# Rotary embedding on one core: half a row less of a cast ahead of the copy that releases a store

## The chip, the core and the metric

The kernel runs on one core of a Trainium2 chip. Its time is the device time of one execution in microseconds (us). Before the change the median of three runs is 161.36 us (161.2 to 161.51).

## The reference

Each row of x has 16 heads of 64 numbers. The first 32 of a head (x1) are turned against the last 32 (x2) by an angle that depends only on the row's place in the sequence:

```python
batch, seq, dim = 16, 512, 1024        # x is float32; cos and sin are [512, 32]
x = x.reshape(batch, seq, num_heads, head_dim)
x1, x2 = x[..., :half_dim], x[..., half_dim:]
rotated = np.concatenate([x1 * cos - x2 * sin, x1 * sin + x2 * cos], axis=-1)
```

So 33.5 MB are read, 33.5 MB are written, and there are a few operations for each number.

## The kernel before

**Tiling.** Two batches make a slab: 8 rows of 1024 numbers on each of 128 partitions, 8192 float32 numbers (32 KB) a partition, 4 MB in all. There are 8 slabs, 0 to 7. Two slabs make a pair, and SBUF has three places for a pair (a tile each, named `pair`). Pairs 0-1, 2-3 and 4-5 have a place of their own; pair 6-7 comes into the place of pair 0-1, so its load must wait until store 0-1 has landed.

**The work of a slab.** It is done inside the slab's own place. ScalarE casts the float32 numbers to bf16 into the lower half of the slab (`cast`). VectorE multiplies by the sine table into the upper half, then by the cosine table in the lower half (both line 170), and adds the two with the halves of each head exchanged (line 173). ScalarE then copies the bf16 result of the upper half back over the whole slab as float32 (`copy_out`). Both ScalarE steps go through the helper `copy`, so all of them have line 154. The tables are built once, at the start, with a few small matmuls.

**Transfers.** SP issues all loads and stores through the helper `issue` (line 66), in program order: load 0, the two tables, load 1, loads 2-3 and 4-5 as one transfer each, all within the first 4.3 us; then store 0-1, load 6-7, stores 2-3, 4-5 and 6-7, each of these in two halves (even partitions, then odd ones) of 4 MB.

**Order around the change.** ScalarE's and SP's orders are written out by hand (`keep_in_program_order`). Each pass of the loop first casts the next slab and then copies out its own: in the pass of slab 1, ScalarE casts slab 2, and then copies slab 1 (on which VectorE's three operations have run) in two pieces. The piece held back is the last row (`LAST[1]`, 1024 numbers a partition), and between the two pieces ScalarE casts the first `PART` numbers of slab 3. Store 0-1 waits for the last row. The rest of slab 3's cast comes at the start of the next pass (slab 2), and VectorE's work on slab 3 waits for all of that cast. Pair 2-3 has a like arrangement: the last 512 numbers of slab 3's copy (`LAST[3]`) come only in the pass of slab 4, and store 2-3 waits for them.

The lines that carry this:

```python
    LAST = {1: dim, 3: dim // 2}
...
                    cast(v, PART if v[0] == 3 else 0)
...
            copy_out(u, 0, n * dim - LAST[s])
            cast((3, 0, rpp), 0, PART)
            copy_out(u, n * dim - LAST[s])
```

Of the kernel before, what the change touches and what calls it, by code (L numbers as in the profile page):

```python
# [2 lines left out]

# [4 lines left out]


@with_exitstack  # L10
def kernel(
    ctx: ExitStack,
    tc: tile.TileContext,
    x: bass.AP,
    cos: bass.AP,
    sin: bass.AP,
    num_heads: int,
    out: bass.AP,
):
    nc = tc.nc  # L20
    P = nc.NUM_PARTITIONS

    batch, seq, dim = x.shape
    nh = num_heads
    hd = dim // nh
    half = hd // 2
    bf16 = mybir.dt.bfloat16
    f32 = mybir.dt.float32

    nb = 2  # L30
    nslabs = batch // nb
    rpp = nb * seq // P
    W = rpp * dim
    TP = seq // (2 * rpp)
    TS = P // TP
    TW = 2 * rpp * half

    out_flat = out.rearrange("b s h d -> b s (h d)")

    singles = ctx.enter_context(tc.tile_pool(name="singles", bufs=1))  # L40
    pairs = ctx.enter_context(tc.tile_pool(name="pairs", bufs=3))
    psum = ctx.enter_context(tc.tile_pool(
        name="psum", bufs=1, space=bass.MemoryType.PSUM))


    def view(t, offset, *dims):
        return dataclasses.replace(t, offset=t.offset + offset,
                                   ap=[t.ap[0], *[list(d) for d in dims]])

    places = [pairs.tile([P, 2 * W], f32, tag="pair", name="pair") for _ in range(3)]


    def here(s, n=1):
        return view(places[s // 2 % 3], s % 2 * W, (1, n * W))


    def there(t, s, n=1):  # L60
        return bass.AP(tensor=t.tensor, offset=t.offset + s // 2 * 2 * P * W + s % 2 * W,
                       ap=[[2 * W, P], [1, n * W]])


    def issue(out, in_):
        tc.keep_in_program_order(nc.sync.dma_start(out=out, in_=in_))  # L66


    def load(s, n=1, parts=slice(None)):
        issue(here(s, n)[parts], there(x, s, n)[parts])  # L70


    def store(s, n=1, parts=slice(None)):
        issue(there(out_flat, s, n)[parts], here(s, n)[parts])


    EVEN, ODD = slice(0, P, 2), slice(1, P, 2)


    load(0)  # L80


    cos_sb = singles.tile([P, TW], f32, tag="cos_sb")
    sin_sb = singles.tile([P, TW], f32, tag="sin_sb")
    for t, src in ((cos_sb, cos), (sin_sb, sin)):
        nc.vector.memset(t, 0.0)  # L86
        issue(t[::TS], bass.AP(
            tensor=src.tensor, offset=src.offset, ap=[[TW, TP], [1, TW]]))

    load(1)  # L90
    for s in (2, 4):
        load(s, 2)


    pick = singles.tile([P, 2 * P], bf16, tag="pick")
    nc.gpsimd.memset(pick, 0.0)  # L96
    for g in range(2):
        part = view(pick, g * P, (TP, P // TP), (1, TP))
        nc.gpsimd.affine_select(  # L99
            out=part, in_=part, compare_op=mybir.AluOpType.not_equal,  # L100
            fill=1.0 - 2.0 * g, base=0, pattern=[[0, P // TP], [-TS, TP]],
            channel_multiplier=1)

    tab1 = singles.tile([P, 2 * TW], bf16, tag="tab1")
    for i, t in enumerate((cos_sb, sin_sb)):
        nc.vector.tensor_copy(out=view(tab1, i * TW, (1, TW)), in_=t)  # L106

    accs, tabs = [], []
    for h in range(2):
        acc = psum.tile([P, 2 * rpp * hd], f32, tag=f"acc{h}", name="acc")  # L110
        for i in range(2):
            for f in range(2):
                nc.tensor.matmul(  # L113
                    view(acc, i * rpp * hd + f * half, (hd, rpp), (1, half)),
                    view(pick, i * f * P, (1, P)),
                    view(tab1, i * TW + h * rpp * half, (half, rpp), (1, half)),
                    start=True, stop=True)
        accs.append(acc)
        tabs.append(singles.tile([P, 2 * rpp * hd], bf16, tag=f"tab{h}", name="tab"))
    nc.vector.tensor_copy(out=tabs[0], in_=accs[0])  # L120

    PART = 2 * dim
    LAST = {1: dim, 3: dim // 2}
    passes = []
    for s in range(nslabs):
        r = 0
        for n in {0: (4, 4), nslabs - 1: (4, 2, 2)}.get(s, (rpp,)):  # L130
            passes.append((s, r, n))
            r += n


    def halves(u):
        s, r, n = u
        t = here(s).bitcast(bf16)
        return [view(t, (2 * r + i * n) * dim, (1, n * dim)) for i in range(2)]


    def cast(u, a=0, b=None):
        s, r, n = u
        m = (n * dim if b is None else b) - a
        copy(view(halves(u)[0], a, (1, m)), view(here(s), r * dim + a, (1, m)))


    def copy_out(u, a=0, b=None):
        s, r, n = u
        m = (n * dim if b is None else b) - a
        copy(view(here(s), r * dim + a, (1, m)), view(halves(u)[1], a, (1, m)))  # L150


    def copy(out, in_):
        tc.keep_in_program_order(nc.scalar.copy(out=out, in_=in_))  # L154


    for i, u in enumerate(passes):
        s, r, n = u
        if i == 0:
            cast(u)  # L160
            cast(passes[1])
            copy(tabs[1], accs[1])
            cast(passes[2])
        elif s > 0 and not r:
            for v in passes:
                if v[0] == s + 1:
                    cast(v, PART if v[0] == 3 else 0)
        lo, up = halves(u)
        for t, a in ((up, 0), (lo, rpp * hd)):
            nc.vector.tensor_mul(  # L170
                out=t, in0=lo,
                in1=view(tabs[s % 2], a + r * hd, (hd, n), (0, nh), (1, hd)))
        nc.vector.tensor_add(  # L173
            out=up, in0=up, in1=view(lo, half, (hd, n * nh), (-half, 2), (1, half)))

        if s == 1:
# [3 lines that stand above are left out]
            for act in (store, load):  # L180
                for parts in (EVEN, ODD):
                    act(0 if act is store else 6, 2, parts)
        elif s == 3:
            copy_out(u, 0, n * dim - LAST[s])
        else:
            copy_out(u)
        if s == 4:
            copy_out((3, 0, rpp), rpp * dim - LAST[3])
            for parts in (EVEN, ODD):
                store(2, 2, parts)  # L190
        elif s > 4 and s % 2 and r + n == rpp:
            for parts in (EVEN, ODD):
                store(s - 1, 2, parts)


# [1 line left out]
_INS = ['x', 'cos', 'sin', 'num_heads']  # L197
_OUTS = [((16, 512, 16, 64), 'float32')]

_NUMBERS = {'num_heads': 16}  # L200


# [26 lines left out]
```

## Time and profile before

| What | Number |
|---|---|
| time, median of three runs | 161.36 us |
| the profiled execution: its time | 161.71 us |
| the profiled execution: its span | 159.9 us |
| ScalarE (ACT) busy | 114.3 us, 71% of the span |
| VectorE (DVE) busy | 109.6 us, 69% |
| TensorE (PE) busy | 1.9 us, 1% |
| bytes moved by DMA | 67.24 MB, 420 GB/s over the span |

The profile is of one execution. Its span runs from the first to the last instruction; its time is 1.8 us longer, with what lies around the span. Times within the profile count from the span's start. "Busy" says how long an engine had work, not whether anyone waited for that work; that is read from the chain of waits and from the landing times of the transfers. Transfers are issued by SP, which takes about half a us for each; the bytes move afterwards, on 16 DMA engines, and a transfer's time "to landing" runs from its issue to the moment when its last byte is there, with whatever it stood in the queue.

### The profile page before, as it was taken

To read this page: it belongs to the slowest core of one execution; us is meant where nothing else is said; L and a number is where in the kernel's file an instruction comes from. 1 tells how busy PE (TensorE), PEld (TensorE's weight loads), DVE (VectorE), ACT (ScalarE), POOL (GpSimd) and SP (SyncE) were. 2 spreads that over 40 slices of the span, in tenths; PEclk is the share of its full clock that TensorE was granted. 3 is DMA by queue.
4 is the path that set the end of the run, shared out by engine and by line. 5 is a ranking of instruction groups with operands and counts; after the bars stand their busy time and mean duration, and the time that the engine had idled before them with its cause. 6 is when DMAs were issued, how large, how long until landed. Compare 5 with 4: busy or idle time off the path is not lost.

```text
span 159.9 us, 176 instructions
## 1 busy us (share of the span) xinstructions
PE 1.9 (1%) x8; PEld 1.1 (1%) x8; DVE 109.6 (69%) x38; ACT 114.3 (71%) x27; POOL 1.1 (1%) x7
## 2 busy tenths in 40 slices
PE   0004000000000000000000000000000000000000
PEld 0002000000000000000000000000000000000000
DVE  2004899999806998999899999909999998000000
ACT  3008949992499999999999995699999969400000
POOL 2000000000000000000000000000000000000000
DMA  7999999979989697996996996996996996997966
GB/s 262 393 393 443 500 402 524 475 311 524 410 377 524 262 524 311 475 525 279 508 525 262 525 524 262 525 508 279 524 508 279 524 492 295 525 443 344 525 262 262
DMA packets 1472, 67.24 MB, mean 420 GB/s; under 512 B 256, under 2 KB 256, under 8 KB 320
## 3 DMA queue, kind: packets, MB, share of 16 engines
q1 hardware_dynamic: 1472, 67.24, 98.0%
HBM read 33.69 MB, written 33.55 MB: 420 GB/s over the span
## 4 chain that ended last, share of the span: by engine, by line
DMA 51%; DVE 14%; ACT 12%; issue 6%; ACTq 2%; SPq 1%
DMA pair<-in_x_dram 36%; DMA out_dram<-pair 15%; ACT pair L154 12%; DVE pair L170 10%; DVE pair L173 4%; ACTq L224 1%; SPq L66 1%; DVE sin_sb L86 0%; DVE cos_sb L86 0%; ACTq L154 0%
## 5 line engine op out<-in xcount | busy, mean ns | idle before, releaser
L154 ACT CAST pair<-pair 128x8192 bf16<-128x8192 f32 (+10 forms) x25 | 112.2, 4557 | 22.7 <-DMA pair<-in_x_dram 21.3
L170 DVE TENSOR_TENSOR pair<-pair,tab 128x8192 bf16<-128x8192 bf16 (+2 forms) x22 | 71.4, 3258 | 12.4 <-ACT pair L154 12.0
L173 DVE TENSOR_TENSOR pair<-pair 128x8192 bf16<-128x8192 bf16 (+2 forms) x11 | 35.8, 3259 | 0.3
L106 DVE CAST tab<-cos_sb 128x512 bf16<-128x512 f32 x1 | 0.4, 426 | 11.1 <-DMA cos_sb<-in_cos_dram 11.1
L113 PE MATMUL acc<-tab,pick 128*128 128x256 bf16 x8 | 1.9, 412 | 13.5 <-DVE tab L106 13.5
L120 DVE CAST tab<-acc 128x1024 bf16<-128x1024 f32 x1 | 1.2, 1225 | 1.0 <-PE acc L113 1.0
L154 ACT ACT_TABLE_LOAD x1 | 1.3, 1283 | 0.7 <-PEq L210 0.7
L113 PEld LDWEIGHTS <-pick 128*128 128x128 bf16 x8 | 1.1, 137 | 13.8 <-issue 12.0
L86 DVE MEMSET cos_sb<- 128x512 f32 x1 | 0.5, 485 | 0.9 <-PEq L210 0.9
L154 ACT CAST tab<-acc 128x1024 bf16<-128x1024 f32 x1 | 1.0, 1005 | 0.0
L99 POOL TENSOR_SCALAR_AFFINE_SELECT pick<-pick 128x128 bf16<-128x128 bf16 x2 | 0.6, 308 | 0.1
L86 DVE MEMSET sin_sb<- 128x512 f32 x1 | 0.5, 485 | 0.1
L106 DVE CAST tab<-sin_sb 128x512 bf16<-128x512 f32 x1 | 0.4, 419 | 0.0
L96 POOL MEMSET pick<- 128x256 bf16 x1 | 0.3, 311 | 0.3 <-POOLq L210 0.3
L210 POOL MEMSET const-bfloat16-1.0<- 128x1 bf16 x1 | 0.1, 101 | 0.0
L210 POOL MEMSET const-uint8-127<- 128x1 uint8 x1 | 0.1, 101 | 0.0
L210 POOL MEMSET const-float32-0.0<- 128x1 f32 x1 | 0.1, 98 | 0.2 <-issue 0.2
L210 POOL MEMSET const-float32-1.0<- 128x1 f32 x1 | 0.1, 98 | 0.0
## 6 DMA issues: line engine op xcount, KB each, us to landing
pair<-in_x_dram SPq DMA_DIRECT2D x2, 4096.0 KB, 16.1
out_dram<-pair SPq DMA_DIRECT2D x8, 17.9
cos_sb<-in_cos_dram SPq DMA_DIRECT2D x1, 64.0 KB, 11.5
sin_sb<-in_sin_dram SPq DMA_DIRECT2D x1, 64.0 KB, 11.1
pair<-in_x_dram SPq DMA_DIRECT2D x4, 29.1
```

Of the source, the lines that this page charges most:

```text
L66: tc.keep_in_program_order(nc.sync.dma_start(out=out, in_=in_))
L86: nc.vector.memset(t, 0.0)
L96: nc.gpsimd.memset(pick, 0.0)
L99: nc.gpsimd.affine_select(out=part, in_=part, compare_op=mybir.AluOpType.not_equal, fill=1.0 - 2.0 * g, base=0, pattern=[[0, P // TP], [-T ...
L106: nc.vector.tensor_copy(out=view(tab1, i * TW, (1, TW)), in_=t)
L113: nc.tensor.matmul(view(acc, i * rpp * hd + f * half, (hd, rpp), (1, half)), view(pick, i * f * P, (1, P)), view(tab1, i * TW + h * rpp * ...
L120: nc.vector.tensor_copy(out=tabs[0], in_=accs[0])
L154: tc.keep_in_program_order(nc.scalar.copy(out=out, in_=in_))
L170: nc.vector.tensor_mul(out=t, in0=lo, in1=view(tabs[s % 2], a + r * hd, (hd, n), (0, nh), (1, hd)))
L173: nc.vector.tensor_add(out=up, in0=up, in1=view(lo, half, (hd, n * nh), (-half, 2), (1, half)))
L210: nc = _bacc.Bacc("TRN2", target_bir_lowering=False, num_devices=1)
L224: with _tile.TileContext(nc) as tc:
```

## The change

One line. ScalarE casts the first 1536 numbers of slab 3 (one and a half rows) instead of the first 2048 (two rows) between the two pieces of the copy of slab 1. The rest of the cast, in the next pass, has 6656 numbers instead of 6144. The number and the order of instructions stay as they were on all engines; only these two sizes differ.

```diff
-    PART = 2 * dim
+    PART = 3 * dim // 2
     LAST = {1: dim, 3: dim // 2}
```

## The prediction

> **What bounds the kernel now.** I read the profile in this order: the DMA queue, the chain of waits, then stretches of time, because the last two seem to say different things. The queue's row on the page:
>
> ```profile
> q1 hardware_dynamic: 1472, 67.24, 98.0%
> ```
>
> One queue moves all 67.24 MB, and its packets fill 98.0% of the time of 16 DMA engines. The chain that ended last (start, length, what):
>
> ```profile
> 49.12 8.91 ACT pair L154 x3
> 58.04 0.02 issue
> 58.05 0.53 SPq L66
> 58.58 0.04 issue
> 58.62 23.34 DMA out_dram<-pair
> 81.96 0.02 issue
> 81.98 0.02 SPq L66
> 82.00 0.04 issue
> 82.04 19.12 DMA pair<-in_x_dram
> ```
>
> It runs through exactly the edited place: the three ScalarE pieces from 49.12 (seven rows of slab 1 out, two rows of slab 3 in, the last row of slab 1 out), then store 0-1, then load 6-7. Taken literally, a store issued earlier ends everything earlier. But the 23.34 us run from the issue to the landing, and a packet that waits its turn counts in them. So I ask when the transfers landed (the DMA view of three single issues, the last number being us to landing): load 4-5, issued at 3.79; the first half of store 0-1, issued at 58.05; and the very first load, issued at 0.74, which has nothing ahead of it.
>
> ```profile
> pair<-in_x_dram SPq DMA_DIRECT2D x1, 58.6
> ```
> ```profile
> out_dram<-pair SPq DMA_DIRECT2D x1, 14.1
> ```
> ```profile
> pair<-in_x_dram SPq DMA_DIRECT2D x1, 4096.0 KB, 12.0
> ```
>
> Load 4-5 lands at 3.79 + 58.6 = 62.4, that is 4.35 us after the store was issued. The store's first half (4 MB) lands at 58.05 + 14.1 = 72.1, its second at 58.62 + 23.34 = 81.96. The rest of the kernel but the last 8 MB, cut at those and the later landing times (columns: stretch, length, then each engine's busy time, clock, DMA share, GB/s):
>
> ```profile
> 42.17:49.10 6.93, 0.00 (x0) 0.00 (x0) 1.06 (x1) 6.90 (x1) 0.00 (x0) 1.00 1.03 435
> 49.10:62.41 13.31, 0.00 (x0) 0.00 (x0) 13.09 (x3) 13.31 (x5) 0.00 (x0) 1.00 0.98 404
> 62.41:81.96 19.55, 0.00 (x0) 0.00 (x0) 18.26 (x6) 19.55 (x4) 0.00 (x0) 1.00 0.99 429
> 81.96:101.16 19.20, 0.00 (x0) 0.00 (x0) 19.03 (x5) 16.07 (x4) 0.00 (x0) 1.00 1.01 437
> 101.16:120.52 19.36, 0.00 (x0) 0.00 (x0) 14.87 (x4) 19.28 (x5) 0.00 (x0) 1.00 1.00 433
> 120.52:139.83 19.31, 0.00 (x0) 0.00 (x0) 14.71 (x10) 15.89 (x5) 0.00 (x0) 1.00 1.00 434
> ```
>
> Each stretch from 62.41 on moves 8 MB in 19.2 to 19.55 us with a DMA share of 0.99 to 1.01: the engines have no gap to close. From the landing of load 4-5 to the last landing at 159.10 are 96.69 us for ten transfers of 4 MB, 9.67 each. **The bytes bound the kernel**, one after the other; the chain goes through the store because its wait is the last one named, not because the DMA engines stood idle for it.
>
> **The change, step by step.** ScalarE's order stays; two of its pieces change size. The rows, by form (busy, mean ns):
>
> ```profile
> L154 ACT CAST pair<-pair 128x7168 f32<-128x7168 bf16 x1 | 6.2, 6160 | 0.0
> ...
> L154 ACT CAST pair<-pair 128x2048 bf16<-128x2048 f32 x3 | 5.6, 1892 | 0.0
> L154 ACT CAST pair<-pair 128x6144 bf16<-128x6144 f32 x1 | 5.3, 5306 | 0.0
> ...
> L154 ACT CAST pair<-pair 128x1024 f32<-128x1024 bf16 x1 | 1.0, 1039 | 0.0
> ```
>
> 1. *The cast ahead of the last row* goes from 2048 to 1536 elements. No row has 1536; both neighbours do (1039 ns at 1024, 1892 at 2048), the middle is 1466. So it ends 1893 - 1466 = 0.43 us earlier. Bounds: 0 and 0.85 (as short as the 1024 form).
>
> 2. *The copy of the last row* (1039 ns) starts at 56.56 in place of 56.99 and ends at 57.60, and both halves of store 0-1 are issued from 57.62, 0.43 earlier. SP has nothing else to do there: its next instruction, the first half of load 6-7, waits for that store's first half to land.
>
> 3. *The rest of the cast of slab 3* goes from 6144 to 6656 elements. Between 5306 and 6160 (at 7168) the middle is 5733, so +0.43. Steps 1 and 3 add up to 1466 + 5733 = 7199 ns where 1893 + 5306 = 7199 were: the cast of slab 3 ends at 63.24 as before, and VectorE starts on slab 3 (63.27) as before. No instruction is added, no wait either. If the sum were off by some tenths, who would notice? ScalarE works from 42.20 to 98.09 without a pause, so an error goes on to the end of that chain, the 512 elements for which store 2-3 waits. That store is issued at 98.11 and its first half lands 12.8 us later; 12.0 is what a half takes with an empty queue. So 0.8 us are covered there, and each tenth above costs a tenth. The forms lie on a line to 0.01 us, so I take 0; the ends are -0.02 and +0.02.
>
> 4. *What 0.43 us of an earlier store are worth.* The cover: with nothing ahead of it, the first half issued at 58.05 would land 12.0 us later, at 70.1; it landed at 72.1, behind load 4-5. At least 2.0 us of it was standing in the queue, so 0.43 more only makes it stand longer. Worth nothing here; the upper bound is the whole 0.43. If the cover were gone (load 4-5 landing 2 us earlier), each tenth would count. Load 6-7 waits for the store's landing, which stays, and so does everything behind it.
>
> Sum: 0 on the profiled execution (span 159.9 us, 161.71 with what lies around it). That execution is 0.35 above the median 161.36 of the three runs; I carry the 0 over to the median: **161.4**.
>
> **What the queue may still do.** One row is odd: between 49.10 and 62.41 the engines moved 404 GB/s, where 429 to 437 is the rule. At 434 those 13.31 us would have been 12.4, so 0.9 us were lost. In the trace's packets of load 4-5 (64 KB, usually 2.42 us each) the last five on each engine are longer, the very last (started at 58.9 to 59.3) by 0.25 on average and 0.39 at most. Part of that lies behind the issue of the store, and could depend on it.
>
> **The rivals.**
>
> *Faster: the chain is right.* If the store's first packets did not have to wait for load 4-5, the 0.43 would come through whole: 161.36 - 0.43 = 160.93. For it: the chain, and the store's long way of 23.34. Against it: the 4.35 us between issue and the landing of the load, the 2.0 us of cover, and ten transfers at 9.67. The Trainium skill speaks for this side (DMA: Bandwidth & Descriptors, Rules for kernel authors): to overlap DMA with compute, issue the DMA early. By that rule the time would be this rival's; the trace agrees only where the queue would run dry, and no row here shows that it does at 58. Chance 0.09.
>
> *Slower: the queued store stretches the load ahead of it.* The mechanism: a packet of load 4-5 is slowed while store descriptors already stand behind it. Priced evenly, the 0.9 us lost over 4.35 us of such company make 0.2 per us, so 0.43 more of it costs 0.09, too little to be told from nothing. It decides only as a step: the last store was issued at 137.83 and its first packet began at 138.96, 1.1 later, so store 0-1 stands in the queue from about 59.15 now, inside the spread in which the engines start their last packet of the load (58.92 to 59.31). After the change it is there at 58.73, ahead of all of these; if by that one more packet on the slowest engine takes the 0.39, the time is 161.36 + 0.39 = 161.75. The point is an issue before about 57.8; 57.62 is past it. For it: the 0.39. Against it: the slow packets begin at 48.8, nine us ahead of the store, and the last load, with stores 2-3 queued behind it at 98.11, has the fastest row of all (437). Chance 0.14. A sister of it would be that ScalarE's copies themselves slow the DMA writes; the row of 437 has ScalarE and VectorE busy for 16 and 19 of 19.2 us, and the moved half row would bring no more than a part of 0.43. The Trainium skill (SBUF — State Buffer, SBUF: two separate sides) says that a compute operation cannot slow a DMA; the rows from 62.41 on agree, the row of 404 has no explanation by it.
>
> *The change does not do what it says*: the issue stays at 58.05 for want of some other semaphore. It was issued 0.02 after the last row's copy ended (56.99 + 1.04 = 58.03), so I give this almost nothing, and its time is also 161.4.
>
> **How the numbers follow.** No change: 0.77, with a range of its own of 161.1 to 161.65 (the three runs spread over 0.31, and the lost 0.9 us of load 4-5 is not a fixed amount). The two rivals hold 0.09 (160.93) and 0.14 (161.75). The range takes both in, since the upper bound of step 4 is the lower rival: 160.9 to 161.8. A measurement of this kernel can tell about 0.2%, 0.32 us, from no change; both rivals lie just beyond that. So faster 0.09, within 0.77, slower 0.14.
>
> **What would show it.** In the profile after: a 1536 form at about 1466 ns and a 6656 form at about 5733; the store's issue at about 57.62 less or plus what load 2-3's landing moved; its way to landing longer by as much as it was issued earlier (14.5 in place of 14.1); ten landings at 9.67 after load 4-5. Wrong if the first half of the store lands earlier relative to load 4-5 (the faster rival), or if the stretch up to the landing of load 4-5 falls clearly below 404 GB/s again and again (the slower one).

## The result and the profile after

The changed kernel takes 161.61 us in the median of 20 runs (161.3 to 162.07), the kernel before 161.33 in 20 (161.09 to 161.73). The ratio is **1.0018, with a 95% interval of 1.001 to 1.0026**: a small loss of 0.28 us, inside the 0.2% that the forecast called no change, but on the slow side of 1.

The edit itself did what the steps say. ScalarE's two changed forms in the profile after (busy, mean ns):

```profile
L154 ACT CAST pair<-pair 128x6656 bf16<-128x6656 f32 x1 | 5.7, 5732 | 0.0
...
L154 ACT CAST pair<-pair 128x1536 bf16<-128x1536 f32 x1 | 1.5, 1466 | 0.0
```

5732 + 1466 = 7198 ns, as before. The chain of waits after, in the same place (start, length, what):

```profile
49.10 8.49 ACT pair L154 x3
57.59 0.02 issue
57.61 0.52 SPq L66
58.13 0.04 issue
58.17 24.00 DMA out_dram<-pair
82.17 0.02 issue
82.19 0.02 SPq L66
```

The store is issued at 57.61, 0.44 earlier, and yet its second half lands at 82.17 where it landed at 81.96. Its way to landing grew by 0.66 (24.00 for 23.34), more than the 0.44 that an unmoved landing would give. The loss lies ahead of it. Load 4-5, issued at 3.78 (the DMA view of that one issue), and the stretch that ends with its landing at 62.69 (columns as in the prediction):

```profile
pair<-in_x_dram SPq DMA_DIRECT2D x1, 58.9
```
```profile
49.10:62.69 13.59, 0.00 (x0) 0.00 (x0) 13.28 (x3) 13.59 (x5) 0.00 (x0) 1.00 0.97 386
62.69:82.17 19.48, 0.00 (x0) 0.00 (x0) 18.32 (x5) 19.48 (x4) 0.00 (x0) 1.00 0.99 431
```

The load lands 0.3 later than in the first profile of before, at 386 GB/s instead of 404 in that stretch; from there on everything runs as before, 431 GB/s and a full queue.

**Where in the stretch?** The DMA view can be cut to the 2.0 us in which all 16 engines begin their last packet of load 4-5 (58 to 60). It then lists 16 packets, and its last column, packet time as a share of 16 engines' 2.0 us, times 2.0 us is the mean length of such a packet; an undisturbed one of 64 KB gives 120.9%, 2.42 us. The kernel before, then after:

```profile
q1 hardware_dynamic: 16, 1.05, 133.4%
```
```profile
q1 hardware_dynamic: 16, 1.05, 160.4%
```

2.67 us before and 3.21 after. One packet on each engine, the last of the load, became longer by half a us, with a store issued ahead of it in both kernels and 0.44 earlier in the changed one. That is where the slower rival had been put.

### The profile page after: what moved, and what is told of

Read it like the earlier page. It is cut to its first block, busy times and chain, and to the rows that moved or that the text cites. A ratio compares the mean times of both kernels' runs of the same rounds, so it can differ in the third digit from the quotient of the medians.

```text
span 160.2 us, 176 instructions
## 1 busy us (share of the span) xinstructions
PE 1.9 (1%) x8; PEld 1.1 (1%) x8; DVE 109.6 (68%) x38; ACT 114.3 (71%) x27; POOL 1.1 (1%) x7
## 4 chain that ended last, share of the span: by engine, by line
DMA 51%; DVE 14%; ACT 12%; issue 6%; ACTq 2%; SPq 1%
DMA pair<-in_x_dram 36%; DMA out_dram<-pair 15%; ACT pair L154 12%; DVE pair L170 10%; DVE pair L173 4%; ACTq L224 1%; SPq L66 1%; DVE sin_sb L86 0%; DVE cos_sb L86 0%; ACTq L154 0%
## 5 line engine op out<-in xcount | busy, mean ns | idle before, releaser
L154 ACT CAST pair<-pair 128x8192 bf16<-128x8192 f32 (+11 forms) x25 | 112.2, 4557 | 23.0 <-DMA pair<-in_x_dram 21.6
```

## The experiments

The theory to test, called the step theory: if the store is in an engine's queue before that engine begins the load's last packet, this packet is long by 0.5 to 1.2 us; if the store comes later (but before the queue runs dry), the packet is not. What the profiles show is the store's issue, and its lead: the time from the issue to the start of these packets. Its rivals: the loss grows evenly with the time that the store stands there (gradual); the loss comes from ScalarE's new pieces and not from the store's issue (ScalarE); load 4-5 varies by itself (chance).

**1 to 2. The two kernels once more, for a second profile each** (no edit).

> The kernel before, unchanged, for a second profile: in the first one the packets of load 4-5 from 48.8 us on were long by themselves, so that their last one began late. Step theory: with a steady load the last packets begin at 58.2 to 58.8, at most 0.7 us after the store's issue at 58.1, and are clean (2.42 us). Chance theory: 0.25 again or more.

> The changed kernel, unchanged, for a second profile. Step theory: the store is issued at about 57.6, 0.6 to 1.2 us ahead of the last packets, and these are long by 0.4 to 0.8 us on average. Chance theory: anything from 0 to 0.8.

Same cut, the kernel before again, then the changed one again:

```profile
q1 hardware_dynamic: 16, 1.05, 125.1%
```
```profile
q1 hardware_dynamic: 16, 1.05, 164.2%
```

2.50 us and 3.28 us. In the kernel before, 12 of the 16 engines were clean (at most 0.04 us long) and four 0.27 to 0.37 long; in the changed one all 16 were 0.66 to 1.14 long. Load 4-5 came steadily this time in the kernel before: the packets ahead of the last, which had been 0.05 to 0.22 long on average in its first profile, were all 2.42. So some of that first excess may have been load 4-5 varying by itself. This varying is not the change's doing: in both profiles of the changed kernel the packets were long already ahead of 55.2, where the two kernels first differ. The last packet is another matter. In these two new profiles the lead goes with it: 0.18 to 0.64 in the kernel before (issue 58.07, starts 58.25 to 58.71), 0.84 to 1.36 in the changed one (57.58, 58.42 to 58.94). But the lead alone does not set the size. The first profile of the kernel before had a lead of 0.87 to 1.26 (58.05, 58.92 to 59.31), as long as the changed kernel's, and its last packets were only 0.25 long; and the four long ones of its second profile are not those with the longest lead.

**3. No row ahead of the last row.**

```diff
-                    cast(v, PART if v[0] == 3 else 0)
+                    cast(v)
...
-            cast((3, 0, rpp), 0, PART)
```

> Nothing of slab 3 is cast ahead of slab 1's last row: the store is issued at about 56.25 and is in the queue at about 57.35, one packet ahead of the last. Step theory: the last packet as in the changed kernel (about 3.2 us), the one before it as ever, time 161.6 to 161.9, not clearly above the changed kernel. Gradual theory: 1.8 us more company than before at 0.65 per us, 162.5. Chance theory: 161.3.

162.16 us, ratio 1.0047 (1.003 to 1.0064), with the store issued at 56.41:

```profile
q1 hardware_dynamic: 16, 1.05, 181.0%
```

3.62 us for the last packet; the last but one (begun at 55.84 to 56.34) stayed at 2.42, although the store was issued while it was moving. The last packet is longer than the 3.2 us that the step theory gave, and 162.16 is above its 161.9, but below the 162.5 of the gradual one.

**4. One row.**

```diff
-    PART = 2 * dim
+    PART = dim
```

> One row of slab 3 ahead of the last row: the store is issued at about 57.2, 1.1 to 1.6 us ahead of the start of the last packets (58.3 to 58.8). Step theory: last packet stretched by 0.8 to 1.2 us, the packets ahead of it not; time between the changed kernel and the one with no rows, 161.7 to 162.1. Gradual theory in any form that slows more than the last packet: the last but one is long too.

161.88 us, 1.003 (1.0017 to 1.0044), issued at 57.28; last packet 3.38 us (169.2% in the same cut), the ones ahead 2.42. As expected by the step theory.

**5. Three rows.** `PART = 3 * dim`.

> Three rows of slab 3 are cast ahead of slab 1's last row, so store 0-1 is issued at about 58.9 and is in the queue at about 60.0, after every engine has begun its last packet of load 4-5 (58.9 to 59.3 in the profile before). Step theory (a store that is in the queue before the load's last packet begins stretches that packet by about 0.8 us on each engine, and one that comes later does not): last packet of load 4-5 at 2.42 to 2.5 us, time 161.0 to 161.3. Gradual theory (each us of company costs the same, 0.28 us measured for 0.43 us, 0.65 per us): 0.85 us less company, 160.8. ScalarE theory (the sizes of ScalarE's pieces matter, not the store's issue): no telling, no order with the issue time. Chance theory (load 4-5 varies by itself): same as before, last packet anywhere between 2.4 and 3.2.

Issued at 59.09. The last packet is clean:

```profile
q1 hardware_dynamic: 16, 1.05, 121.0%
```

But the time was not below before: 161.46 us, 1.0005 (0.9985 to 1.0024). The profile shows a second place to look at. At the next change of direction, from store 0-1 to load 6-7, the last packets of the store (begun between 77.4 and 79.4, the same cut there) are long now:

```profile
q1 hardware_dynamic: 16, 1.05, 132.9%
```

That is 2.66 us, 0.24 long, with 0.08 more in the packets after them. In the profile after, the cut there gives 120.9%; in the second profile of before it gives 132.1%. So against the first profile of before, what the clean first change saves is lost at the second; against the second profile it saves only 0.08 there, too little to show in the time.

**6. Two and a half rows.** `PART = 5 * dim // 2`.

> Two and a half rows: the store is issued at about 58.5 and is there at 59.6, after all last packets of load 4-5 have begun, also where these begin late (58.9 to 59.3). Step theory: their extra length is 0.00 to 0.02 on every engine; the last packets of store 0-1 take 0.2 to 0.3 instead, as with three rows; time as before, 161.2 to 161.5, the best of the row of sizes or level with the kernel before. Gradual theory: 0.43 us less company, 161.1.

161.41 us, 1.0013 (0.9995 to 1.003), issued at 58.48: last load packet 2.42 (121.2%), last store packet 2.67 (133.6%). The packets are as the step theory has them, the time not to be told from before.

**7. Four rows.** `PART = 4 * dim`.

> Four rows of slab 3 ahead: the store is issued at about 59.8 and is there at about 60.9, just as the engines end load 4-5 (60.7 to 61.2). Step theory: last packet 2.42 us; a gap of 0 to 0.3 us may open; time 161.2 to 161.6. Cover as in the prediction (2.0 us after 58.05, so up to 60.05): nothing lost by the issue itself.

161.86 us, 1.0026 (1.0014 to 1.0038), issued at 59.84. The last load packet is nearly clean (122.9%, 2.46 us), and no gap opens behind it; but the last packets of store 0-1 take 2.92 us (145.9%). The time is above what I expected. The largest excess that the profile shows is at that second change of direction, but load 4-5 was slow by itself in this execution too (its last packets began at 58.67 to 59.08, where a steady load has 58.2 to 58.8), so what the whole loss is made of isn't shown.

**8. Six rows.** `PART = 6 * dim`: the cover is taken away.

> Six rows of slab 3 ahead: the store is issued at about 61.4, after load 4-5 has ended (60.7 to 61.2), and its first packets begin at about 62.5. The cover is gone: last packet 2.42 us, then a gap of 1.3 to 1.8 us on the DMA engines; time 162.5 to 163.2. If nothing were lost in spite of it, the transfers would not bound the kernel.

164.71 us, 1.0204 (1.0185 to 1.0223), issued at 61.66. Three stretches around the end of load 4-5:

```profile
58.00:61.20 3.20, 0.00 (x0) 0.00 (x0) 3.17 (x2) 3.20 (x2) 0.00 (x0) 1.00 0.76 328
61.20:62.80 1.60, 0.00 (x0) 0.00 (x0) 1.59 (x1) 1.60 (x2) 0.00 (x0) 1.00 0.00 0
62.80:65.00 2.20, 0.00 (x0) 0.00 (x0) 1.53 (x1) 2.20 (x2) 0.00 (x0) 1.00 1.12 477
```

The DMA engines stand still (0 GB/s) for 1.96 us each on average; the last load packets are clean (120.9%), the last packets of store 0-1 are 0.72 long and the last ones of load 6-7 1.15 long (store 2-3 was issued 1.6 us ahead of them). That is 3.8 us in all, of which 3.3 show in the time, which is above the 163.2 that I had expected at most. Below two rows an earlier store costs; at four and six a later one does.

**9. ScalarE as in the changed kernel, the store later.** SP issues store 0-1 behind a small load of its own that waits for VectorE; the store and load 6-7 are written behind it in the order.

```diff
+    gate = singles.tile([16, 128], f32, tag="gate")
...
+        if s == 2:
+            nc.vector.tensor_copy(out=gate, in_=lo[0:16, 0:128])
+            issue(gate, bass.AP(tensor=cos.tensor, offset=cos.offset, ap=[[128, 16], [1, 128]]))
+            for act in (store, load):
+                for parts in (EVEN, ODD):
+                    act(0 if act is store else 6, 2, parts)
```

> ScalarE does exactly what it does in the changed kernel (1536, last row, 6656), but SP issues store 0-1 only behind a small load (8 KB of the cosine table into a tile of its own) that waits for VectorE's second multiplication of slab 2; so the store is issued at about 58.9 in place of 57.61. Step theory: the last packet of load 4-5 is 2.42 us again, time 161.2 to 161.5, below the changed kernel. ScalarE theory: the last packet is stretched as in the changed kernel (about 3.2), time 161.6 or more.

161.39 us, 1.0009 (0.9992 to 1.0027), issued at 59.01, with ScalarE's pieces of 1536 and 6656:

```profile
q1 hardware_dynamic: 16, 1.05, 121.2%
```

The last packets are clean with the changed kernel's ScalarE: its pieces are not the cause. That rests on the packets; by its time this run can't be told from the changed kernel, whose interval is 1.001 to 1.0026.

**10. ScalarE as before, a store early.** Slab 0's part of store 0-1 is issued as soon as slab 0 is copied out.

```diff
+        if i == 1:
+            for parts in (EVEN, ODD):
+                store(0, 1, parts)
...
-                    act(0 if act is store else 6, 2, parts)
+                    act(1, 1, parts) if act is store else act(6, 2, parts)
```

> ScalarE's order and sizes are those of the kernel before; store 0-1 is split by slabs, and the two halves of slab 0's store are issued as soon as slab 0 is copied out (about 37), some 25 us ahead of the end of load 4-5. Step theory: only the last packet of load 4-5 is stretched, to about 3.2 us; time 161.6 to 162.0. Gradual theory: 21 us more company at 0.65 per us, over 170, and all eight packets of load 4-5 long. ScalarE theory: ScalarE is as before, so 161.3 and a last packet as before (2.4 to 2.8).

As a time this run says nothing: 197.54 us, 1.224 (1.2218 to 1.2263), since other work now waits for slab 0's store to land (VectorE 9.9 us, and ScalarE 36.7 us for VectorE), and the queue runs dry later. All theories missed that. Its packets still answer, because the stores were in the queue from 37 on. All packets of load 4-5 take 2.42 us but the last, which takes 3.38, and ScalarE does nothing at all in that stretch (in the second line the fourth of the five engine columns, ScalarE's, is 0.00):

```profile
q1 hardware_dynamic: 16, 1.05, 169.1%
```
```profile
58.30:61.70 3.40, 0.00 (x0) 0.00 (x0) 3.40 (x1) 0.00 (x0) 0.00 (x0) 1.00 1.08 347
```

A store that has stood there for 21 us costs the same one packet, and not 14 us: the gradual theory falls, and so does the ScalarE theory.

**11. The other store behind a load.** Slab 3 is copied out in one piece, without the 512 numbers held back.

```diff
-        elif s == 3:
-            copy_out(u, 0, n * dim - LAST[s])
...
-            copy_out((3, 0, rpp), rpp * dim - LAST[3])
```

> The other place where a store stands behind a load: slab 3 is copied out in one piece, so store 2-3 is issued at about 84 instead of 98.1 and stands 14 us behind load 6-7. Store 0-1 is as before. Step theory: the last packet of load 6-7 (97.6 to 98.3 in the profile before, 2.42 us) is stretched to about 3.2 us, time 161.8 to 162.2. Gradual theory: 14 us at 0.65, about 170. ScalarE theory and chance theory: 161.2 to 161.4, last packet 2.42.

162.4 us, 1.0055 (1.0034 to 1.0076), with store 2-3 issued at 84.08. The cut at the last packets of load 6-7 (97 to 99):

```profile
q1 hardware_dynamic: 16, 1.05, 163.4%
```

Both profiles of the kernel before, with store 2-3 issued at 98.1, have this line there:

```profile
q1 hardware_dynamic: 16, 1.05, 120.9%
```

So 3.27 us in place of 2.42. The same thing at another place, 40 us later and between other slabs.

**12. Load 6-7 held back as well.** Based on the kernel before: load 6-7 waits behind a small load that waits for VectorE's sum of slab 3 (the tile `gate` again, in the pass of slab 3).

> Based on the kernel before (two rows). The other change of direction: load 6-7 is held back, by a small load (8 KB) that waits for VectorE's sum of slab 3, from 71.4-72.2 to about 77.5, so that it comes into the queue only as the engines begin the last packets of store 0-1 (77.6 to 78.3). In the runs so far these store packets were 0.2 to 0.7 us long wherever the load's last packets ahead were clean. Step theory, taken to this place too: both changes of direction are clean, all packets 2.42, time 160.9 to 161.2. If the load's company is not the cause there: 161.3 to 161.6, the last packets of store 0-1 0.2 to 0.5 long as in the kernel with three rows.

162.34 us, 1.006 (1.0034 to 1.0086), from 161.41 to 163.5. Not the better version that I had hoped for. Its profile has clean last packets of store 0-1 (2.42), but also a load 4-5 that was slow by itself and last packets of it that are long (2.69), so that the condition (a clean first change) was not met, and six engines' first packets of load 6-7 are 0.06 to 0.94 long. What makes this kernel slow is not settled.

The sizes in one view, by the store's issue:

| Rows ahead | Store 0-1 issued | Its lead over the last load packets | These packets, mean | Last packets of store 0-1, mean | Ratio (95%) |
|---|---|---|---|---|---|
| 0 | 56.41 | 1.86 to 2.35 | 3.62 | 2.42 | 1.0047 (1.003 to 1.0064) |
| 1 | 57.28 | 0.87 to 1.50 | 3.38 | 2.42 | 1.003 (1.0017 to 1.0044) |
| 1.5 (after) | 57.61 | 0.86 to 1.36 | 3.21 | 2.42 | 1.0018 (1.001 to 1.0026) |
| 2 (before, first profile; load slow) | 58.05 | 0.87 to 1.26 | 2.67 | 2.42 | 1 |
| 2 (before again) | 58.07 | 0.18 to 0.64 | 2.50 | 2.64 | 1 |
| 2, load 6-7 held back (load slow) | 58.10 | 0.67 to 1.00 | 2.69 | 2.42 | 1.006 (1.0034 to 1.0086) |
| 2, slab 3 in one piece | 58.11 | 0.16 to 0.61 | 2.42 | 2.61 | 1.0055 (1.0034 to 1.0076) |
| 2.5 | 58.48 | -0.17 to 0.22 | 2.42 | 2.67 | 1.0013 (0.9995 to 1.003) |
| 1.5, store gated | 59.01 | none | 2.42 | 2.68 | 1.0009 (0.9992 to 1.0027) |
| 3 | 59.09 | none | 2.42 | 2.66 | 1.0005 (0.9985 to 1.0024) |
| 4 | 59.84 | none | 2.46 | 2.92 | 1.0026 (1.0014 to 1.0038) |
| 6 | 61.66 | none, a gap | 2.42 | 3.14 | 1.0204 (1.0185 to 1.0223) |

Where the load is called slow, the packets ahead of its last ones were long too; that holds for both profiles of the changed kernel and for four rows as well. The time of the row with slab 3 in one piece is lost at load 6-7 (experiment 11). Held by the issue, the table is in order: 57.61 and earlier long, 58.05 to 58.11 between, 58.48 and later clean. Held by the lead, it isn't quite: in three executions with a slow load, leads of 0.67 to 1.00 and 0.87 to 1.26 went with packets 0.27 and 0.25 long, and leads of 0.86 to 1.36 with 0.79.

No version beat the kernel before.

## Why the prediction was right in its number and wrong in a step

**What held.** The time (161.61) lies in the range and in the forecast's own 161.1 to 161.65. Steps 1 to 3 came out to within 1 ns and 0.01 us: 1466 and 5732 ns, the issue at 57.61; the two casts of slab 3 add up as before. That the transfers bound the kernel held, and so did reading the landings instead of the chain: 0.44 of an earlier store brought no earlier landing. That there is a cover held too: at 59.84 no gap opens, at 61.66 one of 1.96 us does. Its size of 2.0 us (up to an issue at 60.05) was read in an execution whose load 4-5 was late, and so was the run at 59.84. With a steady load the cover is shorter, by the run with six rows: its engines end the load at 60.94 on average, and the store's first packets begin 1.24 us after the issue, so a store from about 59.7 on would leave a gap.

That the number held is partly luck: the longer packets, 0.8 us on each engine, show only as 0.28 in the median.

**What failed is step 4**: "so 0.43 more only makes it stand longer. Worth nothing here", with bounds of nothing and a gain. Standing in the queue was not free. With the store issued 0.84 to 1.36 us before the last load packets begin, these took 3.21 and 3.28 us in the two profiles of the changed kernel, against 2.67 and 2.50 in those of the kernel before and 2.42 for a clean one, and the median rose by 0.28. Bounding the step only on the gain's side was the mistake; the price of waiting was left to a rival.

**The slower rival was the right mechanism, and its point fits.** It put the point at an issue of about 57.8: at 57.61 and earlier all engines are hit by 0.5 us or more, at 58.05 to 58.11 the mean is 0 to 0.27, at 58.48 none is hit. The reason for the point does not fit: by it a store is in the queue 1.1 us after its issue, in the changed kernel at 58.71, and eight of the sixteen engines had begun their last packet by then; these were as long as the others. Its price was built wrongly: not one more packet of 0.39 on the slowest engine, but the same last packet, by about 0.8, on all of them. Both reasons that I set against it were misread. The slow packets from 48.8 on come and go from one execution to the next: the second profile of before has none of them, and the last packets are long without them (one row, no rows). And the clean last load with stores 2-3 behind it was no counterexample: those are issued at 98.11 while the last packets begin at 97.63 to 98.35, too late to hurt; issued at 84 they do (experiment 11). In the even version of the rival, company would cost 0.2 us for each us; it costs one packet, whether it lasts 1 us or 21.

**The faster rival** had its 0.09 for a queue that does not stand in the way. The Trainium skill (DMA: Bandwidth & Descriptors, Rules for kernel authors) says, for overlapping DMA with compute, to issue the DMA early. Here, where the queue stays full, the runs differ from it: 0.8 us earlier costs 0.3%, 1.6 us earlier 0.47%.

**The sister of the slower rival**, ScalarE slowing the DMA writes, is out by experiments 9 and 10. The Trainium skill (SBUF — State Buffer, SBUF: two separate sides) has it that compute cannot slow a DMA; the long packets beside an idle ScalarE agree, as far as ScalarE goes (VectorE was busy in all of that stretch).

**What stays open.** Why a store in the queue lengthens the packet ahead of it, no run shows. How far ahead it must be issued isn't shown either: with a steady load the packets are long at leads from 0.87 on, and clean at leads up to 0.64 on all but four engines, yet the two executions with a slow load and issues at 58.05 and 58.10 do not fit a limit in between. Why the change of direction back (store to load) is clean after a long first one and 0.2 to 0.7 long after a clean one isn't settled either; in the traces the engines begin those packets 0.66 to 0.98 us apart where they are clean, 0.13 to 0.61 apart where they are long, which is no more than seen together. It is likely part of the answer to why 0.8 us of longer packets cost 0.28 in the median. Another part may be that the two profiled executions of the changed kernel (162.02 and 162.08) are among its longest: in both, load 4-5 was slow already ahead of its last packet, by 0.2 us, and the usual one may also lose less at that packet. No trace of a usual one is at hand.

## What to carry to other kernels

Where the DMA queue never runs dry, look at when transfers land, not at the chain through their issue; and do not take a wait in the queue to be free. In this kernel a store issued well before the last packet of the load ahead of it had begun (at 57.61 or earlier, for starts from 58.15 on) made that packet up to half as long again on average (3.6 us for 2.42); the cheapest issues (58.05 to 59.09) lay 1.6 to 2.7 us ahead of the first engine's end of a steady load (60.7), late enough for the load's last packet and early enough for the 1.2 us that pass from issue to first packet. A small piece of work held back ahead of a store can therefore be a timer, and moving it is a change of timing even when no engine's work grows.

## What the runs showed of the hardware that was not expected

- A load's last 64 KB packet on each engine took 2.42 us where no store was issued ahead of its start, and 3.21 to 3.62 us on average with a store issued 0.84 us or more ahead of it (load 4-5, issues at 57.61 and earlier; load 6-7, issue at 84.08). With the issue at 58.05 or 58.10 and a slow load it took 2.67 and 2.69 us. With a steady load the packets before it stayed at 2.42 even with the store there for 21 us.
- From the issue of a store on an empty queue to its first packets 1.2 us passed (61.66 to 62.85, six rows; the issue itself takes 0.53 of them), and its 4 MB had landed 11.4 us after the issue.
- Loads vary by themselves: the same load 4-5 landed 57.8 and 58.6 us after its issue in two executions of the same kernel. Its packets from about 48.8 us on, ahead of the last, are long in 5 of the 14 profiles.
